# A two-layer transformer block: the feed-forward in the planner's order, weight transfers behind gate rows, the residual factor inside the residual, and adds moved between two engines

## Chip, cores and metric

The kernel runs on one core of a Trainium2 chip. The time is device microseconds from launch to end, and smaller is better. A core has TensorE (PE, the matmuls), VectorE (DVE), ScalarE (ACT), GpSimd (POOL) and SyncE (SP, whose queue issues nearly all transfers). Each works through a list of instructions of its own in order and waits for the others by semaphores.

## What is computed

A two-layer block over 512 latent tokens and 256 context tokens of width 1024, in float32. Cut to what matters here:

```
for i in range(2):
    mods = silu(c) @ w_ada[i] + b_ada[i]          # shifts, scales, gates (latent); the same for the context
    hx = x * (1 + sc1) + sh1
    ax = window_attention(hx) if i == 0 else differential_attention(hx)   # ends in a product with wo
    x  = layer_norm(alpha * x + g1 * ax, ln1_g, ln1_b)
    h  = x * (1 + sc2) + sh2
    fx = square(relu(h @ w1)) @ w2                # w1 1024x4096, w2 4096x1024
    x  = layer_norm(alpha * x + g2 * fx, ln2_g, ln2_b)
    # layer 0 does the same to the context tokens; layer 1 leaves them out
return x
```

`alpha` is 4 ** 0.25.

## The kernel before

**Tiles.** The 768 tokens are six blocks of 128 (`tb` 0 to 5; blocks 4 and 5 are context; layer 1 ends with four). Each product is made in three matmuls (lines 330, 331, 332) from a rounded half and a remainder of both operands. So each weight tile that a transfer brings as `w_raw` is cast on ACT to `w_h` and split on DVE to `w_l` (`wsplit`, lines 313 and 319), and activations likewise.

**Feed-forward.** `mlp_pipe` forms `h` for the w1 tiles 0 to 5 plainly (the function `plain`, with `relu`, its square and the split `hid`), and then the tiles q = 3 to 15 in pairs with sums of operands (`hx_sum`, `w_half`), one matmul tile fewer a pair. Products with w2 (`y_ps`) run between them; their sums are kept in `fx`. In layer 0 the tensor `acc`, which holds the LayerNorm's result, takes the residual early: `residual` (from `R0.step`) multiplies by a row of `lnrow` and adds another, and the result is spilled to memory and loaded again for the end. At the end `last_y` forms the last products. `fold` multiplies `fx` by the gate row `g` and adds it to `acc` on POOL, 24 operations; `gated_add` multiplies the last product by the gate (`g_tmp`) and adds it to `acc`. Then `stats`, `moments` (with `rstd`, a power on POOL) and `normalise` (line 540) on DVE make the LayerNorm, and `ln_job` transposes each block on PE (`xn_t`, eight transposes, line 555) and writes the next operand (`hx0m`, `hx` or `hx1m`).

**What sets the order.** A planner, `Flow`, runs through generators (jobs) while the program is built. It holds a model time `fl.T` of PE and of four more engines. A job yields a condition, and goes on when the model says that it holds; the first job that can go on is taken. PE's instructions stand exactly in the planner's order. For ACT ("A"), DVE ("D") and POOL ("G") the planner keeps a queue too, but its order binds only while `fl.pin` names the engine; otherwise the compiler's scheduler sets it. Before, "DAG" is pinned in both attentions and nothing in the feed-forwards, including the LayerNorms at their ends. `LNLAT` is what the planner adds to the end of a normalise before it lets PE transpose. An operation that carries no `ins` is planned but never pinned.

**Transfers.** All go through `dma` on SP's queue. `queue["behind"]` names an instruction behind which the following transfers must stand. Before, `plain` asks for its w1 tile (`wsplit(t["w1"][l, ft])`) at the moment of use, and the compiler places it.

**Residual rows.** The rows `g` of `lnrow` are loaded again over the gate rows (`reload`), then multiplied by alpha on DVE (`scale_inplace`, a `TENSOR_SCALAR` on 128x1024); this happens to two rows in each layer.

Of the kernel before, what the change touches and what calls it, by code (L numbers as in the profile page):

```python
# [240 lines left out]
def hybrid_block(ctx: ExitStack, tc: tile.TileContext, t: dict, out: bass.AP):  # L241
# [63 lines left out]
    def wsplit(src, n=1024, raw=None, hl=None, pool=False):  # L305
# [8 lines left out]
        a = fl.op("A", act(n), [q, hg], ins=last["cast"])  # L314
# [3 lines left out]
        else:  # L318
            last["split"] = nc.vector.tensor_tensor(**kw)  # L319
# [379 lines left out]
    def scale_inplace(ap, s):  # L699
        dv(D // 2, [], nc.vector.tensor_scalar, out=ap, in0=ap, scalar1=s, scalar2=None, op0=ALU.mult)  # L700

    def mlp_pipe(l, hx, ready, ntok, acc, get_gates, done, fx, T, R):
# [252 lines left out]
        def last_y():  # L955
            def final(half, tb, pt, p, slot):
                r = gated_add(R.pool, lambda x: sm_.give(slot, x), acc[tb], half, pt, p, gates[0 if tb < NXB else 1],
                              half == 1 if l else half == 0 or tb == ntb - 1)
# [1175 lines left out]
```

## Time and profile before

| | us |
|---|---|
| median of 3 runs (1641.33 to 1644.98) | 1643.1 |
| the profiled execution, whole | 1639.2 |
| its span in the profile | 1637.4 |
| PE busy, share of the span | 96% |
| DVE busy | 70% |
| ACT busy | 48% |
| POOL busy | 26% |
| DMA engines, mean share | 33% |

Times below count from the span's start. In the trace, attention of layer 0 goes to about 302, the second half of its out projection to 345, its feed-forward to 868 (the pairs from 445), LayerNorm and layer 1's products for attention to 915, attention to 1255, out projection and LayerNorm to 1283, and layer 1's feed-forward from 1276 to the end. A timeline row reads: start, duration, engine, source line, operation, output and inputs, shape, and in brackets the idle time of the engine before it and what ended it. A row with "x2" is two instructions together. Durations of neighbours overlap a little, so what one costs its engine is the distance between starts.

### The profile page before, as it was taken

The numbers are of one execution on the slowest core, as the hardware profiler recorded it, in microseconds if no ns is written. First come the engines' busy times: TensorE is split into PE (matmuls) and PEld (weight loads), VectorE is DVE, ScalarE is ACT, GpSimd is POOL, SyncE is SP. The second block draws the span as 40 slices with busy tenths as digits, with TensorE's granted clock in tenths as the row PEclk, the third lists the DMA queues.
The fourth block names the chain that finished last, engine by engine and source line by source line (L and its number), as shares of the span: only waits on it lengthen the run. The fifth ranks groups of instructions, "written<-read, shape, count | busy, mean of one in ns | idle before, by whom it ended". The sixth has DMA issues, their size and how long they took to land.

```text
span 1637.4 us, 25213 instructions
## 1 busy us (share of the span) xinstructions
PE 1571.6 (96%) x9465; PEld 1377.9 (84%) x9465; DVE 1142.4 (70%) x2201; ACT 791.2 (48%) x1679; POOL 433.7 (26%) x369
## 2 busy tenths in 40 slices
PE   7999999989999999999997999999999799999998
PEld 5887677779888888888986999999987788888896
DVE  4655676589686777967576677777765876566667
ACT  3465665365334334333425555556552745544450
POOL 1344453102111211121183122220100123223363
PEclk9999999999999999999998999999999899999999
DMA  9111551533344444444332222211132333333321
GB/s 372 48 53 34 181 175 44 173 118 129 102 146 163 142 132 139 158 139 148 110 133 91 81 71 71 72 49 40 39 107 100 104 116 103 103 103 103 103 68 62
DMA packets 66435, 181.18 MB, mean 111 GB/s; under 512 B 7368, under 2 KB 13320, under 8 KB 66312
## 3 DMA queue, kind: packets, MB, share of 16 engines
q1 hardware_dynamic: 66312, 179.56, 32.6%
q8 instruction: 74, 1.21, 0.3%
q14 instruction: 49, 0.40, 0.1%
HBM read 168.49 MB, written 11.04 MB: 110 GB/s over the span
## 4 chain that ended last, share of the span: by engine, by line
PE 78%; DVE 9%; ACT 5%; POOL 3%; issue 3%; DMA 2%; SPq 0%; DVEq 0%; ACTq 0%; POOLq 0%
PE y_ps L331 9%; PE y_ps L332 9%; PE y_ps L330 9%; PE h_ps L330 7%; PE h_ps L331 7%; PE h_ps L332 7%; PE qkv_ps L330 3%; PE qkv_ps L331 3%; PE qkv_ps L332 3%; PE s_ps L1785 2%; PE o_ps L1395 2%; PE pT_ps L1413 2%; PE o_ps L1823 2%; POOL acc L273 1%; PE q_ps L330 1%
## 5 line engine op out<-in xcount | busy, mean ns | idle before, releaser
L331 PE MATMUL y_ps<-w_l,hid 128*128 128x512 f32 (+1 forms) x648 | 255.0, 393 | 1.6 <-DVE w_l L319 1.6
L330 PE MATMUL y_ps<-w_h,hid 128*128 128x512 f32 (+1 forms) x648 | 255.7, 395 | 0.6 <-DVE fx L267 0.6
L332 PE MATMUL y_ps<-w_h,hid 128*128 128x512 f32 (+1 forms) x648 | 254.9, 393 | 0.0
L319 DVE TENSOR_TENSOR w_l<-w_raw,w_h 128x1024 fp32r<-128x1024 f32 (+1 forms) x133 | 160.1, 1212 | 47.9 <-ACT w_h L313 46.4
L313 ACT CAST w_h<-w_raw 128x1024 fp32r<-128x1024 f32 (+1 forms) x133 | 131.1, 1002 | 104.8 <-PE y_ps L332 76.7
L332 PEld LDWEIGHTS y_ps<-w_h,hid 128*128 128x128 f32 x648 | 122.2, 189 | 28.6
L331 PEld LDWEIGHTS y_ps<-w_l,hid 128*128 128x128 f32 x648 | 122.3, 189 | 27.5 <-DVE w_l L319 2.9
L267 DVE TENSOR_TENSOR w_half<-w_raw,w_half 128x512 fp32r<-128x512 f32 x130 | 105.8, 824 | 54.7 <-ACT w_half L270 54.3
L330 PEld LDWEIGHTS y_ps<-w_h,hid 128*128 128x128 f32 x648 | 122.4, 189 | 25.4 <-DVE fx L267 1.0
L270 ACT CAST w_half<-w_raw 128x512 fp32r<-128x512 f32 x130 | 79.2, 621 | 128.0 <-PE h_ps L332 97.8
L330 PE MATMUL qkv_ps<-w_h,hx 128*128 128x384 f32 (+1 forms) x384 | 128.6, 335 | 3.2 <-ACT w_h L313 3.2
L273 POOL TENSOR_TENSOR w_sum<-w_raw 128x512 f32<-128x512 f32 x26 | 42.7, 1643 | 328.0 <-DMA w_raw<-in_w 265.1
L331 PE MATMUL qkv_ps<-w_l,hx 128*128 128x384 f32 (+1 forms) x384 | 123.6, 322 | 2.5 <-DVE w_l L319 2.5
L273 POOL TENSOR_TENSOR e<-e,sm 128x512 f32<-128x512 f32 (+2 forms) x96 | 93.5, 990 | 112.7 <-DVE sm L267 77.8
L332 PE MATMUL qkv_ps<-w_h,hx 128*128 128x384 f32 (+1 forms) x384 | 122.9, 320 | 0.0
L267 DVE TENSOR_TENSOR fx<-y_ps,fx 128x512 f32<-128x512 f32 x110 | 75.2, 686 | 36.1 <-PE y_ps L332 35.8
L270 ACT ACTIVATE relu<-relu 128x384 f32<-128x384 f32 (+3 forms) x104 | 69.3, 671 | 61.2 <-DVE relu L267 59.9
L273 POOL TENSOR_TENSOR rope<-rope,rope 128x256 f32<-128x256 f32 (+1 forms) x40 | 35.3, 883 | 216.3 <-DVE rope L267 138.8
L273 POOL TENSOR_TENSOR w_raw<-w_raw,w_sum 128x512 f32<-128x512 f32 x26 | 39.1, 1506 | 197.3 <-DVE w_half L267 160.4
L678 DVE CUSTOM_DVE_ANT_0 w_raw<-w_raw,cB 128x512 f32<-128x512 f32 x112 | 84.0, 784 | 4.7 <-PE y_ps L332 4.1
L270 ACT ACTIVATE e<-e,nm 128x513 f32<-128x513 f32 (+2 forms) x96 | 65.9, 687 | 30.8 <-DVE nm L267 26.8
L330 PEld LDWEIGHTS qkv_ps<-w_h,hx 128*128 128x128 f32 x384 | 72.8, 189 | 5.7 <-ACT w_h L313 3.6
(268 smaller groups left out, 4315.1 us busy)
## 6 DMA issues: line engine op xcount, KB each, us to landing
w_raw<-in_w SPq DMA_DIRECT2D x128, 512.0 KB, 3.6
w_raw<-in_w_adaT SPq DMA_DIRECT2D x56, 512.0 KB, 3.8
w_raw<-in_w_ada SPq DMA_DIRECT2D x24, 512.0 KB, 4.0
w_raw<-in_b_w SPq DMA_DIRECT2D x32, 384.0 KB, 3.9
raw<-in_w_ada SPq DMA_DIRECT2D x16, 512.0 KB, 9.6
w_raw<-in_a_wq SPq DMA_DIRECT2D x8, 512.0 KB, 8.7
w_raw<-in_a_wo SPq DMA_DIRECT2D x8, 512.0 KB, 4.2
w_raw<-in_b_wo SPq DMA_DIRECT2D x8, 512.0 KB, 4.5
```

Source lines behind the costliest of these rows:

```text
L267: return fl.op("D", dve(n), deps, lat, fn(**kw))
L270: return fl.op("A", act(n), deps, lat, fn(**kw))
L273: return fl.op("G", us, deps, lat, fn(**kw))
L313: last["cast"] = nc.scalar.copy(out=h[:, :n], in_=raw[:, :n])
L319: last["split"] = nc.vector.tensor_tensor(**kw)
L330: nc.tensor.matmul(out=o, lhsT=lh, rhs=rh, start=start, stop=False, **kw)
L331: nc.tensor.matmul(out=o, lhsT=lh, rhs=rl, start=False, stop=False, **kw)
L332: last["pe"] = nc.tensor.matmul(out=o, lhsT=ll, rhs=rh, start=False, stop=stop, **kw)
L678: i = fn(**kw)
L1395: nc.tensor.matmul(out=po[odd * HD:odd * HD + HD, 0:256], lhsT=vv[:, kb, kvh], rhs=pt_[:, odd * 256:odd * 256 + 256], start=(i == 0), stop ...
L1413: nc.tensor.transpose(out=pp[:, c * P:(c + 1) * P], in_=es[j][:, i * P:(i + 1) * P], identity=ident)
L1785: nc.tensor.matmul(out=sp[:, c * 512:c * 512 + 384], lhsT=qTt[:, tt, hl, qb * P:(qb + 1) * P], rhs=kS[:, tt, c * 384:c * 384 + 384], start ...
```

## The change

- `LNLAT` falls from 6.0 to 0.2, so the planner puts a block's transposes earlier into PE's order.
- `fl.pin` is "DAG" in layer 0's feed-forward. From the end of its plain part on, `fl.loose` leaves out the weights' casts and splits and those of the halves. In layer 1's feed-forward "DAG" holds to the end of the plain part and then nothing is pinned.
- A helper `w1` asks for each w1 tile one tile ahead; the first three of layer 0 must stand on SP's queue behind the gate rows and the `acc` loads.
- `residual` applies alpha itself, in two `SCALAR_TENSOR_TENSOR`, and the four scalings of rows are left out. In layer 0 the residual gets a low priority in the plan.
- Layer 0's last adds of the second half (blocks 0 to 4) go from POOL to DVE, and the planner is told that they come after the folds.

```diff
-LNLAT = 6.0
+LNLAT = 0.2
+LOW = 100
...
-        t.eng, t.us, t.seq = eng, us, self.n
-        for d in deps:
+        t.eng, t.us, t.seq = eng, us, self.n + LOW * self.low
+        for d in flat(deps):
...
-        a = fl.op("A", act(n), [q, hg], ins=last["cast"])
+        a = fl.op("A", act(n), [q, hg], ins=None if fl.loose else last["cast"])
...
-            d = fl.op("D", dve(n), [a], ins=last["split"])
+            d = fl.op("D", dve(n), [a], ins=None if fl.loose else last["split"])
...
+        m = [m, *more]
         if last:
-            return dv(512, [m], nc.vector.tensor_tensor, out=acc[:, cs_], in0=acc[:, cs_], in1=tm, op=ALU.add)
-        return gp(pool2(512), [m], nc.gpsimd.tensor_tensor, out=acc[:, cs_], in0=acc[:, cs_], in1=tm, op=ALU.add)
+            return dv(512, m, nc.vector.tensor_tensor, out=acc[:, cs_], in0=acc[:, cs_], in1=tm, op=ALU.add)
+        return gp(pool2(512), m, nc.gpsimd.tensor_tensor, out=acc[:, cs_], in0=acc[:, cs_], in1=tm, op=ALU.add)
...
-    def residual(acc, g, b, after=None):
-        d = dv(D, [], behind(nc.vector.tensor_tensor, after), out=acc, in0=acc, in1=g, op=ALU.mult)
-        return dv(D, [d], nc.vector.tensor_tensor, out=acc, in0=acc, in1=b, op=ALU.add)
+    def residual(acc, g, b, deps, after=None):
+        d = dv(D, deps, behind(nc.vector.scalar_tensor_tensor, after), out=acc, in0=acc, scalar=ALPHA, in1=g, op0=ALU.mult,
+               op1=ALU.mult)
+        return dv(D, [d], nc.vector.scalar_tensor_tensor, out=acc, in0=b, scalar=ALPHA, in1=acc, op0=ALU.mult, op1=ALU.add)
...
+    def w1(l, ft):
+        if ft < 6 and (l, ft) not in W1:
+            kept = queue["behind"]
+            if l == 0 and ft < 3:
+                queue["behind"] = queue["w1"]
+            W1[l, ft] = wsplit(t["w1"][l, ft])
+            queue["behind"] = kept
+        return W1.get((l, ft))
...
                     if n == 0:
+                        W[ft] = w1(l, ft)
+                        w1(l, ft + 1)
...
-                        W[ft] = wsplit(t["w1"][l, ft])
...
-                              half == 1 if l else half == 0 or tb == ntb - 1)
+                              half == 1 or l == 0, more=[folds[half, tb]])
...
         if l == 0:
             y_weights(0, 1)
+        if l == 0:
+            fl.loose = True
+        else:
+            fl.pin = ""
...
-    fl.pin = ""
+    fl.pin = "DAG"
...
             dma(512, [], out=acc[tb][:, 0:512], in_=y_spill[tb])
+        queue["w1"] = queue["last"]
...
         def done1(tb, st, r):
+            if tb == NTB - 2:
+                fl.low = True
+                w1(0, 0)
+                w1(0, 1)
+                fl.low = False
             fl.add(ln_job(pool, acc[tb], tb, hx, A, B, ready, st, r, fx[tb]), 0)
...
-                d = residual(acc[tb], gx, gc, last["pe"])
+                fl.low = True
+                d = residual(acc[tb], gx, gc, rows + [fl.pe(0.0)], last["pe"])
+                fl.low = False
...
-            for b_, i in ((gx, 0), (gc, 1)):
-                reload(b_, lnrow[0, i:i + 1])
-                scale_inplace(b_, ALPHA)
+            rows[:] = [reload(b_, lnrow[0, i:i + 1]) for b_, i in ((gx, 0), (gc, 1))]
...
-                          LNLAT if tb < NTB - 1 else 2.5), 0)
+                          LNLAT), 0)
...
-    fl.pin = ""
+    fl.pin = "DAG"
...
-        scale_inplace(lb, ALPHA)
...
         def done3(tb, st, r):
+            if tb == NXB - 2:
+                w1(1, 0)
...
-            reload(gx, lnrow[1, 0:1])
-            scale_inplace(gx, ALPHA)
-            res = [lambda tb=tb: residual(acc[tb], gx, lb, last["pe"]) for tb in range(NXB)]
+            row = reload(gx, lnrow[1, 0:1])
+            res = [lambda tb=tb: residual(acc[tb], gx, lb, [row], last["pe"]) for tb in range(NXB)]
```

PE's list has as many matmuls as before. Between the transposes of blocks 4 and 5 behind layer 0's out projection stand 24 `h_ps` matmuls before and 60 now, and at the end of layer 0 block 0's transposes stand 36 `y_ps` matmuls earlier. In layer 1 the transposes come behind 78 `y_ps` matmuls of the out projection, and then 18 and 6 between blocks, where 102 stood ahead of three blocks together.

DVE's list at the last LayerNorm behind layer 0's out projection (`acc_3735` is block 5, `acc_3730` block 0, `g_3736` and `g_3738` the rows); before:

```order
L267 SCALAR_TENSOR_TENSOR acc_3735<-acc_3735,g_tmp 128x512
L678 TENSOR_TENSOR acc_3730<-acc_3730,g_3736 128x1024
L267 BN_STATS bn<-acc_3735 128x6
L267 TENSOR_TENSOR hx0m<-fx,hx0m 128x2x128
L267 TENSOR_SCALAR g_3738<-g_3738 128x1024
L267 BN_AGGR mv<-bn 128x2
L267 TENSOR_TENSOR hx0m<-fx,hx0m 128x2x128
L267 TENSOR_SCALAR rstd<-mv 128x1
L267 TENSOR_TENSOR hx0m<-fx,hx0m 128x2x128
L540 TENSOR_SCALAR acc_3735<-acc_3735,mv,rstd 128x1024
```

and now:

```order
L272 BN_STATS bn<-acc_3735 128x6
L272 TENSOR_TENSOR hx0m<-fx,hx0m 128x2x128
L272 BN_AGGR mv<-bn 128x2
L272 TENSOR_SCALAR rstd<-mv 128x1
L272 TENSOR_TENSOR hx0m<-fx,hx0m 128x2x128 x2
L684 SCALAR_TENSOR_TENSOR acc_3730<-acc_3730,g_3736 128x1024
L545 TENSOR_SCALAR acc_3735<-acc_3735,mv,rstd 128x1024
L272 SCALAR_TENSOR_TENSOR acc_3730<-g_3738,acc_3730 128x1024
```

The scaling of the row (`TENSOR_SCALAR g_3738`) is gone, and the only residual operation left ahead of block 5's normalise is a product between it and its `rstd` step. The w_l splits of w1 tiles, three of which stood together ahead of block 4's normalise, are now spread.

DVE's list where the plain part ends (`w_l` from here on are w2 tiles; `hx0m` with 4x128 are sums that write over part of the operand of the plain part); before:

```order
L267 TENSOR_TENSOR hid<-relu,hid 128x768
L267 TENSOR_TENSOR hx_sum<-fx,hx_sum 128x4x128 x2
L319 TENSOR_TENSOR w_l<-w_raw,w_h 128x1024 x2
L267 TENSOR_TENSOR w_half<-w_raw,w_half 128x512
L319 TENSOR_TENSOR w_l<-w_raw,w_h 128x1024
L267 TENSOR_TENSOR relu<-relu 128x768
L267 TENSOR_TENSOR hid<-relu,hid 128x768
L267 TENSOR_TENSOR hx0m<-fx,hx0m 128x4x128 x3
L319 TENSOR_TENSOR w_l<-w_raw,w_h 128x1024
```

and now:

```order
L272 TENSOR_TENSOR hx_sum<-fx,hx_sum 128x4x128
L272 TENSOR_TENSOR hid<-relu,hid 128x768
L272 TENSOR_TENSOR hx_sum<-fx,hx_sum 128x4x128
L272 TENSOR_TENSOR hx0m<-fx,hx0m 128x4x128 x3
L324 TENSOR_TENSOR w_l<-w_raw,w_h 128x1024 x3
L272 TENSOR_TENSOR relu<-relu 128x768
L272 TENSOR_TENSOR hid<-relu,hid 128x768
L324 TENSOR_TENSOR w_l<-w_raw,w_h 128x1024
```

The three `hx0m` sums moved ahead of the first three w2 splits.

POOL's list at the end of layer 0 (`fx` with a gate row `g`, then `acc` with `fx`, are the folds); before:

```order
L273 TENSOR_TENSOR acc_7899<-acc_7899,fx 128x512
L273 TENSOR_TENSOR acc_7900<-acc_7900,fx 128x512
L273 TENSOR_TENSOR fx<-fx,g_7997 128x512 x2
L273 TENSOR_TENSOR acc_7901<-acc_7901,fx 128x512
L273 TENSOR_TENSOR acc_7902<-acc_7902,fx 128x512
L273 TENSOR_TENSOR acc_7897<-acc_7897,g_tmp 128x512
L273 TENSOR_TENSOR rstd<-rstd,mhalf 128x1
L273 TENSOR_TENSOR acc_7898<-acc_7898,g_tmp 128x512
L273 TENSOR_TENSOR rstd<-rstd,mhalf 128x1
```

and now:

```order
L278 TENSOR_TENSOR fx<-fx,g_7993 128x512 x2
L278 TENSOR_TENSOR acc_7897<-acc_7897,fx 128x512
L278 TENSOR_TENSOR acc_7898<-acc_7898,fx 128x512
L278 TENSOR_TENSOR fx<-fx,g_7995 128x512 x2
L278 TENSOR_TENSOR acc_7899<-acc_7899,fx 128x512
L278 TENSOR_TENSOR acc_7900<-acc_7900,fx 128x512
L278 TENSOR_TENSOR rstd<-rstd,mhalf 128x1 x6
```

The adds of `g_tmp` are gone from POOL, and the six `rstd` follow the last fold directly.

More of the change, by code (lines that the diff above doesn't have):

```diff
@@ L60, in __init__, with flat @@
         self.done, self.ins = None, None
+def flat(x):
+    return [z for y in x for z in flat(y)] if isinstance(x, (list, tuple)) else [x]
 class Flow:
@@ L74, in __init__ @@
         self.events = []
-        self.prev, self.order, self.pin = {}, None, ""
+        self.prev, self.order, self.pin, self.loose, self.low = {}, None, "", False, False
     def pe(self, us):
@@ L521, in reload @@
     def reload(b, src, c0=0):
-        dma(D - c0, [], out=b[:, c0:], in_=src[:, c0:].broadcast_to([P, D - c0]))
+        return dma(D - c0, [fl.pe(0.0)], out=b[:, c0:], in_=src[:, c0:].broadcast_to([P, D - c0]))
     def stats(a, half, dep, st=None):
@@ L583, in hxs, with gated_add @@
         return hx[k // 2][:, k % 2, hl, sl]
-    def gated_add(pool, give, acc, half, pt, p, gate, last, scale=1.0):
+    def gated_add(pool, give, acc, half, pt, p, gate, last, scale=1.0, more=()):
         cs_ = slice(half * 512, (half + 1) * 512)
@@ L752, in half @@
                 w = R.half_tile(nhalf[0] - 1)
-                a = ac(512, [dep, R.rhalf.get()], nc.scalar.copy, out=w[:, 0:512], in_=src)
-                d = dv(512, [a], nc.vector.tensor_tensor, out=w[:, 512:1024], in0=src, in1=f(w)[:, 0:512],
-                       op=ALU.subtract)
+                a = nc.scalar.copy(out=w[:, 0:512], in_=src)
+                a = fl.op("A", act(512), [dep, R.rhalf.get()], ins=None if fl.loose else a)
+                d = nc.vector.tensor_tensor(out=w[:, 512:1024], in0=src, in1=f(w)[:, 0:512], op=ALU.subtract)
+                d = fl.op("D", dve(512), [a], ins=None if fl.loose else d)
                 rel = Task()
@@ L895, in pair @@
             yield from mix(3)
-        gates, st, Wy, fresh = [], {}, {}, set()
+        gates, st, Wy, fresh, folds = [], {}, {}, set(), {}
         def y_weights(c, half, n=2):
@@ L920, in fold @@
             d = gp(pool2(512), [d], nc.gpsimd.tensor_tensor, out=x, in0=x, in1=g[:, cs_], op=ALU.mult)
-            gp(pool2(512), [d], nc.gpsimd.tensor_tensor, out=acc[tb][:, cs_], in0=acc[tb][:, cs_], in1=x, op=ALU.add)
+            folds[half, tb] = gp(pool2(512), [d], nc.gpsimd.tensor_tensor, out=acc[tb][:, cs_], in0=acc[tb][:, cs_], in1=x,
+                                 op=ALU.add)
         def sink(c, half, tb, pt, p, slot):
@@ L957, in final @@
                 r = gated_add(R.pool, lambda x: sm_.give(slot, x), acc[tb], half, pt, p, gates[0 if tb < NXB else 1],
-                              half == 1 if l else half == 0 or tb == ntb - 1)
+                              half == 1 or l == 0, more=[folds[half, tb]])
                 st[tb], r = stats(acc[tb], half, r, st.get(tb))
-                r_half[tb] = r
+                first_half, r_half[tb] = r_half.get(tb), r
                 if half:
-                    done(tb, st[tb], r)
+                    done(tb, st[tb], [first_half, r])
             early, r_half = [], {}
@@ L1029, in last_y @@
                     sm_.give(slot, m)
-                    r = dv(256, [m], nc.vector.tensor_tensor, out=acc[tb][:, cs_], in0=acc[tb][:, cs_], in1=tm, op=ALU.add)
+                    r = dv(256, [m, folds[1, tb]], nc.vector.tensor_tensor, out=acc[tb][:, cs_], in0=acc[tb][:, cs_], in1=tm,
+                           op=ALU.add)
                     r = dv(256, [r], nc.vector.bn_stats, out=parts[:, n + 1], in_=acc[tb][:, cs_])
@@ L1500, in hybrid_block @@
         acc = [apool_top.tile([P, D], F32, name="acc0", tag="acc", bufs=NTB) for _ in range(NTB)]
+        rows = []
         gx, gc = [bcast_load(pool, gate_d[(0, 2)][s:s + 1], f"g1{s}", 512, 2) for s in range(2)]
@@ L1630, in hybrid_block @@
         EB1, XB1, SB = 5, 3, 1
-        fl.prev, fl.pin = {}, "DAG"
+        fl.loose = False
+        fl.pin = "DAG"
         rsk, rsq = Ring(fl, SB), Ring(fl, SB)
@@ L1971, in hybrid_block @@
         fl.run()
-    fl.pin = ""
+    fl.pin = "DAG"
     with tc.tile_pool(name="mlp1", bufs=1, reuse_waits="tile") as pool:
```

1 line of the change is left out of this document (added).

## The prediction

> **What bounds the kernel now.** I read the page first, then the windows by stage, then the waits and the timelines of TensorE (PE) and VectorE (DVE) in the stages where PE is not full.
>
> ```profile
> span 1637.4 us, 25213 instructions
> PE 1571.6 (96%) x9465; PEld 1377.9 (84%) x9465; DVE 1142.4 (70%) x2201; ACT 791.2 (48%) x1679; POOL 433.7 (26%) x369
> 302.50:360.00 57.50, 51.97 (x263) 43.60 (x262) 41.17 (x76) 31.24 (x77) 4.20 (x6) 0.95 0.54 188
> 339.20:399.90 60.70, 55.17 (x351) 53.37 (x350) 57.29 (x79) 34.78 (x70) 10.42 (x5) 0.94 0.34 123
> 445.00:826.00 381.00, 373.75 (x1852) 333.58 (x1851) 283.89 (x538) 148.16 (x237) 69.98 (x47) 1.00 0.44 145
> 826.00:915.00 89.00, 78.41 (x364) 65.91 (x363) 55.58 (x95) 33.27 (x87) 47.37 (x37) 0.94 0.26 89
> 1255.00:1325.00 70.00, 61.05 (x352) 53.35 (x352) 59.65 (x95) 40.16 (x83) 8.39 (x8) 0.93 0.24 78
> 1325.00:1637.40 312.40, 304.54 (x1868) 271.62 (x1867) 204.63 (x275) 143.11 (x253) 114.77 (x72) 1.00 0.29 96
> ```
>
> In a window's row stand its length, the busy time of PE, weight loads, DVE, ScalarE (ACT) and GpSimd (POOL), and the granted clock. PE is busy 1571.6 of 1637.4 us, so all its idle time is 65.8 us. The change adds no matmul and takes none away, so it can only gain idle time and slow clock. Both lie in the three stages round a LayerNorm that feeds PE: out projection into feed-forward of layer 0 (57.50 − 51.97 = 5.53 us idle, clock 0.95), the end of layer 0 (89.00 − 78.41 = 10.59, clock 0.94) and layer 1's LayerNorm before its feed-forward (70.00 − 61.05 = 8.95, clock 0.93). The middle of layer 0's feed-forward (381.00 − 373.75 = 7.25 in 381 us) and layer 1's (7.86 in 312) are nearly full.
>
> **Stage 1: out projection, LayerNorm, first feed-forward tiles (302 to 406).**
>
> ```profile
> 343.19 1.03 PE L555 MATMUL xn_t<-identr,acc 128*128 128x128 f32 x8
> 356.46 1.94 PE L555 MATMUL xn_t<-identr,acc 128*128 128x128 f32 x8 [5.17 <-issue]
> 405.79 0.39 PE L330 MATMUL y_ps<-w_h,hid 128*128 128x512 f32 x1
> 349.80 0.68 DVE L267 SCALAR_TENSOR_TENSOR acc<-acc,g_tmp 128x512 f32<-128x512 f32 x1
> 350.40 1.22 DVE L678 TENSOR_TENSOR acc<-acc,g 128x1024 f32<-128x1024 f32 x1
> 351.54 0.68 DVE L267 BATCH_NORM_STATS2 bn<-acc 128x6 f32<-128x512 f32 x1
> 352.14 0.41 DVE L267 TENSOR_TENSOR hx0m<-fx,hx0m 128x256 fp32r<-128x256 f32 x1
> 353.61 0.69 DVE L267 TENSOR_SCALAR g<-g 128x1024 f32<-128x1024 f32 x1 [1.06 <-DMA g<-in_lnrow]
> 355.55 0.81 DVE L540 TENSOR_SCALAR acc<-acc,mv,rstd 128x1024 f32<-128x1024 f32 x1 [0.44 <-POOL rstd L273]
> 371.43 0.95 DVE L267 TENSOR_TENSOR relu<-relu 128x768 f32<-128x768 f32 x1
> 372.30 1.22 DVE L267 TENSOR_TENSOR acc<-acc,g 128x1024 f32<-128x1024 f32 x1
> 381.57 1.75 DVE L267 TENSOR_TENSOR relu<-relu 128x768 f32<-128x768 f32 x1 [0.23 <-ACT relu L270]
> 383.24 3.49 DVE L267 TENSOR_TENSOR fx<-fx 128x512 f32<-128x512 f32 x2
> 397.55 2.34 DVE L319 TENSOR_TENSOR w_l<-w_raw,w_h 128x1024 fp32r<-128x1024 f32 x2
> ```
>
> The 5.17 us of PE are the last block's LayerNorm: a residual product (350.40), a 1.06 us DMA wait and a scaling (353.61) stand in DVE's queue ahead of its normalise (355.55). After the idle time eight transposes take 1.94 us instead of 1.03. In the changed order the scaling vanishes, the wait for the second row comes behind that normalise, the residual product stands between block 5's rstd step and its normalise, where DVE waits for POOL anyway (0.44), and 60 h matmuls instead of 24 stand between the transposes of blocks 4 and 5. The normalise then starts near 355.55 − 1.06 − 0.6 − 0.44 = 353.4 and ends near 354.2. PE is through with the out projection at 345.4 (343.19, 0.8 of transposes, six matmuls), and block 4's transposes (0.9) and 60 h matmuls of 256 columns at 0.117 (half of a 512's 0.233, below) bring it to 353.3. So of 5.17 some 0.9 stays. PE's own gain by the first y matmul is then the idle 5.53 − 0.9 plus slow clock, 0.05 × 57.5 = 2.9, and a little behind 360: **8 us at most**.
>
> What is late next is DVE. It is busy 57.29 of 60.70 us from 339.20 to 399.90, and the residuals are still to be done before the first w2 splits (397.55, two of them). Counted from the changed order, between the first residual and those splits stand 12 residual operations and 4 w_l splits of 1024 columns, 10 of 768, 25 of 512, 4 of 256 and a normalise (by their rows 0.41 and 0.81 at most, 2.5 together). By start-to-start spacing a 1024 costs 1.14 (350.40 to 351.54), a 768 0.87 (371.43 to 372.30), a 512 0.60 (351.54 to 352.14): 16 × 1.14 + 10 × 0.87 + 25 × 0.60 + 2.5 = 44.4, and 1.14 for the first w2 split, 45.5. From a first residual at about 350.0 (today's is at 350.40, and one split less now stands ahead of it) DVE is through at 395.5. Beside POOL such operations are slower: 383.24 took 3.49 for two (1.2 alone) and 381.57 took 1.75 (0.95), together 3.1. That gives 398.6 for the split and the first y matmul, instead of 405.79: **gain 7.2**. Without contention PE's 8 bounds it; with today's 3.41 us of DVE idle kept as well (60.70 − 57.29) it is 4.0. I take 7.2, since those POOL operations stay. The two scalings that go (0.69 each) are inside this count. The trace has no `scalar_tensor_tensor` of 1024 columns; the 512 one at 349.80 gives way after 0.60, as other 512s do, so twelve of 1024 cost between 1.14 and 1.20 each, 0.7 in all, within these ends. The third DVE piece shown with the change costs PE at least 1.7 us, already covered by the 398.6: the hx0m sums now stand ahead of the w2 splits and need PE's last tile partly read.
>
> The w1 transfers now go behind gate rows and acc loads, so the gate row no longer waits behind three 512 KB transfers. That lets block 0's chain begin earlier. I value it at nothing of its own, since PE does not wait for it in 302 to 345; if a w1 tile came late instead, DVE would have it within the bounds above.
>
> **The middle (406 to 826).**
>
> ```profile
> PE h_ps L330 <- ACT relu L270: 3.1, 2, 1.6
> 462.87 0.44 PE L330 MATMUL h_ps<-hx_sum,w_half 128*128 128x384 f32 x1 [1.48 <-ACT relu L270]
> 656.83 0.44 PE L330 MATMUL h_ps<-hx_sum,w_half 128*128 128x384 f32 x1 [1.61 <-ACT relu L270]
> ```
>
> Pinning DVE, ACT and POOL to the plan moves their rows here by seven places at most, and PE's order is the same. The waits for relu (3.1 in all, two times) can vanish, gain 3, or come in two or three more of the 13 pairs, loss 4.  Value **0**, from −4 to +3.
>
> **Stage 2: end of layer 0 (826 to 915).**
>
> ```profile
> 813.16 0.33 SPq L279 DMA_DIRECT2D w_raw<-in_w  x1
> 826.10 3.27 POOL L273 TENSOR_TENSOR fx<-fx,g 128x512 f32<-128x512 f32 x2 [28.36 <-DMA g<-gate_d]
> 862.23 1.29 POOL L273 TENSOR_TENSOR acc<-acc,g_tmp 128x512 f32<-128x512 f32 x1
> 864.76 0.55 POOL L273 TENSOR_TENSOR rstd<-rstd,mhalf 128x1 f32<-128x1 f32 x1 [1.24 <-DVE rstd L267]
> 868.56 0.60 PE L555 MATMUL xn_t<-identr,acc 128*128 128x128 f32 x4
> 880.23 2.17 PE L555 MATMUL xn_t<-identr,acc 128*128 128x128 f32 x8 [2.76 <-DVE g_tmp L589]
> 892.58 0.45 PE L330 MATMUL qkv_ps<-w_h,hx 128*128 128x384 f32 x1 [2.93 <-ACT w_h L313]
> 894.45 0.69 PE L331 MATMUL qkv_ps<-w_l,hx 128*128 128x384 f32 x1 [1.42 <-DVE w_l L319]
> 869.96 1.84 DVE L540 TENSOR_SCALAR acc<-acc,mv,rstd 128x1024 f32<-128x1024 f32 x1
> 859.67 0.40 PE L331 MATMUL y_ps<-w_l,hid 128*128 128x512 f32 x1
> 859.90 0.39 PE L332 MATMUL y_ps<-w_h,hid 128*128 128x512 f32 x1
> ```
>
> A 512-wide matmul starts every 0.233 us (859.67 to 859.90). Block 0's transposes move 36 matmuls forward, 8.4 us: from 868.56 to 860.2. But POOL does 24 fold operations from 826.10 to 862.23 (1.5 us each), and in the changed order all six rstd stand behind them. So block 0 gets its rstd at 862.23 + 0.55 and its normalise (0.81) ends near 863.9: a **new wait of 3.8**. From there the five removed POOL adds (1.29 each; on DVE about 0.7, and no hand-over) shorten each block's chain. I count the later blocks just in time, the last at about 894, and the two qkv waits (2.93, 1.42) gone, because the weights' cast and split no longer queue behind late blocks. Idle is then 3.8 plus some 0.5, instead of 10.59: gain 6.3. The clock lost 0.06 × 89 = 5.3 us before; after a 3.8 us wait I expect two thirds of it again, gain 1.7. **Gain 8.0**. If the qkv waits stay it is 3.7; if the folds run at the 1.3 us of the add at 862.23, they end at 857 and the new wait is gone: 11.8. I take 8.0, since today's folds run at 1.5.
>
> The clock shows in the transposes: 2.17 us for eight behind a 2.76 us wait. [...]
>
> The adds moved to DVE can meet a fold: at 869.96 a normalise beside a POOL add took 1.84 instead of 0.81. [...]
>
> **Stage 3: layer 1's LayerNorm (1255 to 1325).**
>
> ```profile
> 1276.21 0.58 PE L330 MATMUL h_ps<-hx1m,w_h 128*128 128x256 f32 x1 [1.64 <-ACT hx1m L270]
> 1278.73 0.58 PE L331 MATMUL h_ps<-hx1m,w_h 128*128 128x256 f32 x1 [1.94 <-DVE hx1m L267]
> 1297.51 0.39 PE L330 MATMUL h_ps<-hx1m,w_h 128*128 128x256 f32 x1 [1.52 <-ACT relu L270]
> 1305.42 0.39 PE L330 MATMUL h_ps<-hx1m,w_h 128*128 128x256 f32 x1 [2.03 <-ACT relu L270]
> ```
>
> The transposes of blocks 0 and 1 now stand 24 and 6 y matmuls earlier, so the first h matmuls find their operand nearly ready: of 1.64 + 1.94 I take 2.5 as gone. The relu waits (1.52, 2.03) stay; their order does not change. With 1 us of clock the **gain is 3.5**: 0 if the same chain is merely waited for sooner, 6 if all hx1m waits and half the clock loss of 0.07 × 70 go. Two scalings of 0.69 leave DVE here, inside this value. The rest of layer 1 keeps its order: 0.
>
> **Sum.** 7.2 + 0 + 8.0 + 3.5 = 18.7. The profiled execution took 1639.2 us, so 1620.5; the median of the runs is 1643.1, 3.9 above it, so **1624**.
>
> **Rivals.**
> - A, DVE eats stage 1 (chance 0.12). DVE is at 94% from 339 to 400, and pinned to an order it cannot slip w2 splits ahead; a late second row (it landed at 353.6) would now hold up all behind it. If the first y matmul stays at 405.79, 11.5 remains: 1632. Against it: two scalings are gone, and the row is wanted no sooner than today.
> - B, the fold chain sets stage 2 (0.10). The gate row stands on the SP queue behind a weight transfer (813.16) that waits for a DVE split to free its buffer. If that moves forward less than PE, the new wait grows by up to the 7.2 of stage 1, and 18.7 − 7.2 = 11.5 remains: 1632. For it: POOL's 28 us idle ends with that DMA. Against: the split it hangs on moves with PE.
> - C, slower (0.10). The pins hold ACT's relu behind another operation in each pair of the middle, as at 462.87. There are 13 pairs and two have the wait today. Eleven more of 1.55 and about 1 us of slow clock each make 28; less 18.7, about 9 slower: 1652. It decides from 1.7 us (18.7/11) a pair, clock included. For it: the pins hold in the whole feed-forward except for weights. Against: ACT is busy 148 of 381 us there, and the rows hardly move.
> - D, no change (0.07). The planner's 6.0 us for a LayerNorm was right, and earlier transposes only wait sooner: some 1.5 us at each of the twelve in layer 0 gives back 18 and leaves 1642. Against: by the rows above a product and an add (0.60 each), statistics (0.68), rstd (0.55) and normalise (0.81) make 3.2, near 4 with the small steps, under the 5.6 us of 24 matmuls.
>
> **How the numbers follow.** The forecast has 0.61, with its own range from the bounds: 4.0 − 4 + 3.7 + 0 = 3.7 to 8 + 3 + 11.8 + 6 = 28.8, that is 1614 to 1639. With A and B inside, 1612 to 1640 should hold the time 8 times in 10; most of C and D lies above. About 0.2% (3.3 us) is what a measurement can tell from no change. Faster: forecast, A, B, 0.83; same: D, 0.07; slower: C, 0.10.
>
> **What would show it.** Right: no 5 us wait ahead of block 5's transposes; a first y matmul 6 to 8 us earlier, with DVE full before it; one wait of 3 to 5 us at the first transposes of layer 0's end, behind POOL; no qkv wait for a weight. Wrong: waits for relu in many pairs, a span from first y to first fold that grows, or folds that begin later against PE.

## The result, and the profile after

The changed kernel takes **1628.0 us** (median of 4 runs, 1625.8 to 1628.5) against 1642.4 for the one before in the same comparison: a ratio of 0.9907, 95% interval 0.9890 to 0.9925. That is 14.4 us faster, where 18.7 was worked out; the time lies in the range, 4 us above the number given. The sum came out, but several of its reasons did not, as the experiments show. One of the four executions of pins_off below took 2175.9 us at a granted clock of 0.656, so its median is that of the other three.

The windows of the changed kernel, with the bounds of those shown of before (its line numbers are 5 higher for the same helper lines):

```profile
span 1626.7 us, 25214 instructions
PE 1570.4 (97%) x9465; PEld 1376.0 (85%) x9465; DVE 1144.1 (70%) x2202; ACT 790.2 (49%) x1679; POOL 443.5 (27%) x364
302.50:360.00 57.50, 56.63 (x302) 47.01 (x303) 40.72 (x72) 30.31 (x76) 3.44 (x6) 0.97 0.52 180
339.20:399.90 60.70, 60.70 (x394) 58.82 (x393) 58.01 (x80) 34.01 (x70) 14.09 (x6) 1.00 0.35 126
445.00:826.00 381.00, 372.64 (x1839) 332.49 (x1838) 282.25 (x537) 145.66 (x234) 66.36 (x46) 1.00 0.44 144
826.00:915.00 89.00, 83.61 (x431) 71.76 (x430) 63.85 (x117) 41.46 (x107) 43.17 (x34) 0.96 0.27 89
1255.00:1325.00 70.00, 62.91 (x395) 56.10 (x394) 55.89 (x88) 44.07 (x92) 22.14 (x7) 0.97 0.27 84
```

PE's idle time falls from 5.53 to 0.87 us in the first window, from 10.59 to 5.39 in the one at layer 0's end, and from 8.95 to 7.09 in layer 1's; the clock rises by 0.02 to 0.04 in each. From 339 to 400 us PE now has no idle time at all. DVE is a little fuller than before, 58.01 of 60.70 against 57.29.

PE's timeline shows the main waits that are left (at transposes, at the first w2 product, and the longest of layer 1):

```profile
323.15 1.06 PE L560 MATMUL xn_t<-identr,acc 128*128 128x128 f32 x8 [0.86 <-PE y_ps L337]
357.03 1.04 PE L560 MATMUL xn_t<-identr,acc 128*128 128x128 f32 x8
401.78 0.50 PE L335 MATMUL y_ps<-w_h,hid 128*128 128x512 f32 x1 [0.62 <-ACT w_h L318]
403.04 0.50 PE L336 MATMUL y_ps<-w_l,hid 128*128 128x512 f32 x1 [0.76 <-DVE w_l L324]
864.36 1.97 PE L560 MATMUL xn_t<-identr,acc 128*128 128x128 f32 x8 [4.23 <-DVE acc L545]
1324.46 0.58 PE L335 MATMUL h_ps<-hx_sum,w_half 128*128 128x256 f32 x1 [3.04 <-ACT relu L275]
```

The 5.17 us ahead of block 5's transposes (357.03) are gone. The new wait at block 0's transposes at the end of layer 0 is 4.23 us (3.8 was worked out), and eight transposes behind it take 1.97. POOL's rows say why:

```profile
860.03 2.92 POOL L278 TENSOR_TENSOR acc<-acc,fx 128x512 f32<-128x512 f32 x2
862.91 0.54 POOL L278 TENSOR_TENSOR rstd<-rstd,mhalf 128x1 f32<-128x1 f32 x1
```

The first rstd follows the last fold, and block 0's normalise (DVE `acc`, L545) needs that rstd, as the prediction said.

### The profile page after: what moved, and what is told of

Same layout as the page of the kernel before. It is cut to its first block, busy times and chain, and to the rows that moved or that the text cites. A ratio compares the mean times of both kernels' runs of the same rounds, so it can differ in the third digit from the quotient of the medians.

```text
span 1626.7 us, 25214 instructions
## 1 busy us (share of the span) xinstructions
PE 1570.4 (97%) x9465; PEld 1376.0 (85%) x9465; DVE 1144.1 (70%) x2202; ACT 790.2 (49%) x1679; POOL 443.5 (27%) x364
## 4 chain that ended last, share of the span: by engine, by line
PE 48%; DVE 6%; POOL 4%; ACT 2%; issue 2%; DMA 1%; SPq 0%; DVEq 0%; POOLq 0%; ACTq 0%
PE y_ps L335 6%; PE y_ps L336 6%; PE y_ps L337 6%; PE h_ps L335 5%; PE h_ps L336 5%; PE h_ps L337 5%; PE qkv_ps L335 3%; PE qkv_ps L336 3%; PE qkv_ps L337 3%; PE s_ps L1819 2%; PE o_ps L1857 2%; POOL acc L278 1%; PE pT_ps L1885 1%; POOL w_raw L278 1%; DVE acc L272 1%
## 5 line engine op out<-in xcount | busy, mean ns | idle before, releaser
L278 POOL TENSOR_TENSOR w_raw<-w_raw,w_sum 128x512 f32<-128x512 f32 x26 | 52.4, 2016 | 187.2 <-DVE w_half L773 169.6
L684 DVE CUSTOM_DVE_ANT_0 w_raw<-w_raw,cB 128x512 f32<-128x512 f32 x112 | 90.0, 831 | 15.6 <-PE y_ps L337 13.9
L275 ACT ACTIVATE relu<-relu 128x768 f32<-128x768 f32 (+3 forms) x104 | 69.6, 671 | 49.8 <-DVE relu L272 48.9
```

The lines of the kernel that those rows point to most:

```text
L275: return fl.op("A", act(n), deps, lat, fn(**kw))
L278: return fl.op("G", us, deps, lat, fn(**kw))
L684: i = fn(**kw)
```

## The experiments

Two theories stood at the start. The first: the gain lies in PE's order at the LayerNorms (LNLAT) and the shorter adds. The rival: the pins carry it. To compare stages I use start times of PE's rows in the profiles. **S1** runs from the first matmul of the out projection's second half in layer 0 to the first `y_ps` of its feed-forward; **middle** from there to the gate's transposes (`gate_t`, near 707); **S2** from those to the first `qT_ps` of layer 1's attention; **L1** from layer 1's first out projection matmul to PE's last row. Between S2 and L1 stand 289.7 to 290.6 us in every profile. "Start" is the time at which S1 begins. Times are medians in us; the ratio is to the kernel before, run beside it. Each stage time is from a single profiled execution.

| kernel | time | ratio, 95% interval | start | S1 | middle | S2 | L1 |
|---|---|---|---|---|---|---|---|
| before | 1642.4 | | 302.5 | 103.3 | 301.0 | 208.0 | 424.6 |
| before_again | 1644.7 (one) | | 303.8 | 103.8 | 303.4 | 209.5 | 424.4 |
| changed | 1628.0 | 0.9907 (0.9890 to 0.9925) | 304.1 | 97.7 | 303.1 | 201.1 | 422.9 |
| after_again | 1627.0 | 0.9899 (0.9886 to 0.9913) | 304.7 | 97.1 | 304.2 | 199.4 | 421.7 |
| pins_off | 1626.0 | 0.9896 (0.9881 to 0.9912) | 303.5 | 100.9 | 301.7 | 200.2 | 419.7 |
| pool_adds | 1629.9 | 0.9920 (0.9906 to 0.9935) | 303.3 | 97.0 | 304.8 | 199.8 | 424.0 |
| lnlat_alone | 1647.5 | 1.0022 (1.0012 to 1.0033) | 304.0 | 114.4 | 303.3 | 203.3 | 423.2 |
| w1_back | 1653.1 | 1.0062 (1.0049 to 1.0074) | 302.5 | 119.1 | 303.1 | 199.4 | 430.3 |
| w1_nohold | 1630.5 | 0.9928 (0.9913 to 0.9942) | 303.4 | 101.8 | 304.1 | 200.8 | 421.7 |
| scale_back | 1636.1 | 0.9958 (0.9943 to 0.9973) | 303.4 | 101.4 | 304.5 | 199.1 | 428.1 |
| lnlat_pins_back | 1630.3 | 0.9927 (0.9913 to 0.9940) | 303.7 | 102.3 | 301.3 | 198.1 | 425.6 |
| lnlat_pins_adds_back | 1640.6 | 0.9984 (0.9971 to 0.9997) | 303.5 | 101.3 | 305.8 | 206.6 | 424.2 |
| pin_plain0 | 1623.4 | 0.9879 (0.9866 to 0.9893) | 303.1 | 95.7 | 304.5 | 200.3 | 419.7 |
| plain0_ln2 | 1620.9 | 0.9865 (0.9848 to 0.9881) | 302.1 | 95.7 | 304.0 | 198.2 | 421.2 |

**The two kernels once more (after_again, before_again), no edit.**

> The changed kernel once more, for a second profile. Theory 1 (the gain lies at the LayerNorm stages): median 1626 to 1630, again about 14 us under the kernel before; the first y matmul of layer 0 starts 97 to 98 us after the out projection's second half starts (97.7 in the first profile of the changed kernel, 103.2 in the one of before), and block 0's transposes at the end of layer 0 wait about 4 us. Rival (the first profile was a chance one: its out projection began 1.6 us later than before's and with slow matmuls): that offset differs by more than 1 us here, and the stage times differ by more than 1 us too.

> The kernel before once more, for a second profile, to tell a stage's change from chance. If the 1.6 us by which the changed kernel's out projection of layer 0 starts later is chance, it starts here at 302 to 305 us; if it belongs to the change, at 302.5 again. Stage times: first y matmul 103 us after that start, 301 us more to the gate's transposes at 707, 208 from there to the first transposes of layer 1's queries, within 1 us each.

The time was again under before, by 16 us (14 in the first comparison), and block 0's transposes at the end of layer 0 waited 5.08 us, where about 4 was expected. The start of S1 scatters from 302.1 to 304.7 over all the profiles, before_again's 303.8 among them, so nothing shows that the late start in the first profile of the changed kernel belongs to the change. The middle scatters too, from 301.0 to 305.8, pinned or not. The expectation that each stage repeats within 1 us missed for the middle (2.4) and for S2 (1.5 in the kernel before, 1.7 in the changed one). S1 and S2 repeat within 1 to 2 us, so only differences above that are read below.

**The pins (pins_off).** PE's and POOL's lists stay the same. (`fl.prev` holds the last instruction of each pinned engine; it is emptied where the pins begin again.)

```diff
-    fl.pin = "DAG"
+    fl.pin = ""
     def need(*lms):
...
-        fl.pin = "DAG"
+        fl.prev, fl.pin = {}, "DAG"
...
-    fl.pin = "DAG"
+    fl.pin = ""
     with tc.tile_pool(name="mlp1", bufs=1, reuse_waits="tile") as pool:
```

> The changed kernel with nothing pinned in the feed-forwards, as before; PE's and POOL's lists stay the same, only DVE, ACT and 27 transfers move. Theory 1 (the gain comes from PE's order and the shorter adds, the pins are worth nothing or cost the 1.4 us of waits for w_h and w_l at the first y matmul): 1624 to 1630. Rival 2 (the pins carry the gain, because without them DVE puts residuals and splits ahead of the LayerNorm chains, as before at 350 us): 1633 to 1641, and waits of several us at the transposes of blocks 3 to 5.

1626.0: the pins as a whole are worth nothing in this set, so the rival falls. But two stages move against each other. S1 is 3 to 4 us longer without them, and block 5's transposes wait again, as the row shows. L1 is 2 to 3 us shorter.

```profile
358.06 1.94 PE L560 MATMUL xn_t<-identr,acc 128*128 128x128 f32 x8 [2.54 <-issue]
```

**LNLAT alone (lnlat_alone), made from the kernel before.**

```diff
-LNLAT = 6.0
+LNLAT = 0.2
...
-                          LNLAT if tb < NTB - 1 else 2.5), 0)
+                          LNLAT), 0)
```

> The kernel before with LNLAT 0.2 only: transposes earlier in PE's list, nothing pinned, w1 transfers, scalings and POOL adds as before. Theory 1: the wait of 5.2 us ahead of block 5's transposes shrinks and the stages at the LayerNorms gain part, 1632 to 1639. Rival 2 (without the pins earlier transposes only wait sooner): 1640 to 1648. Rival 3 (LNLAT alone carries all): 1626 to 1631.

1647.5, at the far end of rival 2's range: earlier transposes alone make the kernel slower. S1 is 114.4 instead of 103.5. PE's timeline there:

```profile
327.08 1.94 PE L555 MATMUL xn_t<-identr,acc 128*128 128x128 f32 x8 [5.56 <-DMA acc<-y_spill]
365.37 1.94 PE L555 MATMUL xn_t<-identr,acc 128*128 128x128 f32 x8 [8.91 <-ACT w_h L313]
```

Block 0 waits 5.56 and block 5 waits 8.91. The brackets name a load and ACT's `w_h`, but the transposes need the block's normalised `acc`, and both times they begin within 0.1 us of the end of DVE's normalise (326.97 and 365.27); that `w_h` ended at 364.37. DVE's rows:

```profile
321.37 0.69 DVE L589 TENSOR_TENSOR g_tmp<-y_ps,g 128x512 f32<-128x512 f32 x1 [6.96 <-DMA g<-gate_d]
326.16 0.81 DVE L540 TENSOR_SCALAR acc<-acc,mv,rstd 128x1024 f32<-128x1024 f32 x1
360.43 1.18 DVE L319 TENSOR_TENSOR w_l<-w_raw,w_h 128x1024 fp32r<-128x1024 f32 x1
361.99 0.69 DVE L267 TENSOR_SCALAR g<-g 128x1024 f32<-128x1024 f32 x1 [0.39 <-DMA g<-in_lnrow]
364.46 0.81 DVE L540 TENSOR_SCALAR acc<-acc,mv,rstd 128x1024 f32<-128x1024 f32 x1 [0.44 <-POOL rstd L273]
```

Block 0's chain waits 6.96 us for the gate row, and with DVE unpinned a weight split and the scaling of a row still stand ahead of block 5's normalise. S2 is 203.3 instead of 208.8, so at the end of layer 0 the same edit does win some 5 us.

**The w1 transfers (w1_back, w1_nohold).** First, w1 is asked for at use again; then only the hold behind the gate rows is taken out.

```diff
-                        W[ft] = w1(l, ft)
-                        w1(l, ft + 1)
+                        W[ft] = wsplit(t["w1"][l, ft])
...
-                w1(0, 0)
-                w1(0, 1)
+                pass
...
-                w1(1, 0)
+                pass
```

> The changed kernel with the w1 transfers placed as before, three of them ahead of the gate rows on SP's queue. Theory 1 (revised: earlier transposes are worth nothing in stage 1 unless the gate row and the acc loads come first; in the kernel with LNLAT alone block 0's transposes waited 5.6 us for an acc load): block 0's transposes wait 4 to 6 us here too, 1630 to 1634. Rival (the order of the w1 transfers is worth nothing, the pins hold the rest): 1626 to 1629.

```diff
-            if l == 0 and ft < 3:
-                queue["behind"] = queue["w1"]
```

> The changed kernel with w1 tiles asked for one tile ahead, but without the hold behind the gate rows: only SP's list moves, three 512 KB transfers stand ahead of the gate rows again. Theory 1 (the place on SP's queue matters only for block 0: in the kernel with w1 as before its gate row ended a 6.8 us wait of DVE at 319 and its transposes waited 4.5 us; the other 20 us there came from splits pinned late): out projection to first y matmul 101 to 103 us instead of 97 to 98, 1630 to 1633. Rival (the hold carries the 26 us): 1645 to 1653. Rival (it is worth nothing): 1626 to 1628.

w1_back takes 1653.1, slower than the kernel before, and far outside both expectations. w1_nohold takes 1630.5 with an S1 of 101.8, as expected of the place on SP's queue alone. So the hold is worth some 3 us (1630.5 against 1628.0 and 1627.0) and asking early, with the pins, some 22 (1653.1 against 1630.5). In w1_back the plan puts a tile's cast and split at the moment of use, and the pins hold ACT and DVE to that. PE's rows there, and the window's row:

```profile
378.74 0.45 PE L335 MATMUL h_ps<-hx0m,w_h 128*128 128x384 f32 x1 [1.90 <-ACT w_h L318]
381.37 0.44 PE L337 MATMUL h_ps<-hx0m,w_l 128*128 128x384 f32 x1 [2.02 <-DVE w_l L324]
393.20 0.44 PE L335 MATMUL h_ps<-hx0m,w_h 128*128 128x384 f32 x1 [2.02 <-ACT w_h L318]
394.46 0.44 PE L337 MATMUL h_ps<-hx0m,w_l 128*128 128x384 f32 x1 [0.65 <-DVE w_l L324]
380.00:400.00 20.00, 15.96 (x71) 15.33 (x72) 18.06 (x21) 4.77 (x7) 6.14 (x3) 0.83 0.23 80
```

Two tiles show it here, each with a wait for `w_h` and another for `w_l`, and the clock falls to 0.83 (third number from the end in the window's row, 1.00 in the changed kernel from 339 to 400). Layer 1, where `w1` is edited too, loses 8 us (L1 430.3 against 422.9 and 421.7) with waits for `w_h` and `w_l` as well. Whether it would cost as much without the pins was not run. In w1_nohold the gate row lands late (DVE waits 6.55 for it, 2.61 in the changed kernel), and block 0's transposes wait 4.17:

```profile
320.35 0.69 DVE L594 TENSOR_TENSOR g_tmp<-y_ps,g 128x512 f32<-128x512 f32 x1 [6.55 <-DMA g<-gate_d]
325.09 1.94 PE L560 MATMUL xn_t<-identr,acc 128*128 128x128 f32 x8 [4.17 <-DVE acc L545]
```

**The factor in the residual (scale_back).**

```diff
-    d = dv(D, deps, behind(nc.vector.scalar_tensor_tensor, after), out=acc, in0=acc, scalar=ALPHA, in1=g, op0=ALU.mult,
-           op1=ALU.mult)
-    return dv(D, [d], nc.vector.scalar_tensor_tensor, out=acc, in0=b, scalar=ALPHA, in1=acc, op0=ALU.mult, op1=ALU.add)
+    d = dv(D, deps, behind(nc.vector.tensor_tensor, after), out=acc, in0=acc, in1=g, op=ALU.mult)
+    return dv(D, [d], nc.vector.tensor_tensor, out=acc, in0=acc, in1=b, op=ALU.add)
...
+            for b_, r_ in zip((gx, gc), list(rows)):
+                rows.append(dv(D // 2, [r_], nc.vector.tensor_scalar, out=b_, in0=b_, scalar1=ALPHA, scalar2=None,
+                               op0=ALU.mult))
...
+        scale_inplace(lb, ALPHA)
...
+            row = dv(D // 2, [row], nc.vector.tensor_scalar, out=gx, in0=gx, scalar1=ALPHA, scalar2=None, op0=ALU.mult)
```

> The changed kernel with the residual as two tensor_tensor operations and the four scalings of rows back on DVE. Theory 1 (four times 0.69 us of DVE, two of them in the full stage ahead of the first y matmul, where PE and not DVE ended last by 0.6 us): 0 to 1.5 us, 1626 to 1629. Rival (DVE is the bound there, and pinned scalings wait for the row's transfer with all behind them): 1630 to 1634.

1636.1: 8 to 9 us slower, even more than the rival said. Four scalings are 2.8 us of DVE; the rest is mostly waiting. The plan moves PE's order a little too: 72 `h_ps` matmuls instead of 60 stand ahead of block 5's transposes, which wait 2.85 all the same. DVE's rows of that kernel, one in each layer, and PE's row behind the second:

```profile
355.64 0.69 DVE L272 TENSOR_SCALAR g<-g 128x1024 f32<-128x1024 f32 x1 [2.44 <-DMA g<-in_lnrow]
1273.40 0.69 DVE L272 TENSOR_SCALAR g1x<-g1x 128x1024 f32<-128x1024 f32 x1 [3.78 <-DMA g1x<-in_lnrow]
1274.01 0.69 DVE L272 TENSOR_TENSOR acc<-acc,g_tmp 128x512 f32<-128x512 f32 x1
1274.61 1.22 DVE L324 TENSOR_TENSOR w_l<-w_raw,w_h 128x1024 fp32r<-128x1024 f32 x1
1275.88 0.58 PE L337 MATMUL h_ps<-hx1m,w_l 128*128 128x256 f32 x1 [4.63 <-DVE w_l L324]
```

A scaling waits for its row's transfer, and the add, the statistics and the weight's split that stand behind it on DVE wait too. PE then waits 4.63 us for that split.

**The adds (pool_adds, lnlat_pins_back, lnlat_pins_adds_back).** pool_adds takes the changed kernel and puts the adds back:

```diff
-                              half == 1 or l == 0, more=[folds[half, tb]])
+                              half == 1 if l else half == 0 or tb == ntb - 1, more=[folds[half, tb]])
```

> The changed kernel with layer 0's last five adds on POOL again, behind the folds. Theory 1 (the adds on DVE shorten each block's chain by POOL's hand-over, and are most of stage 2's gain): stage 2 loses 4 to 8 us, 1632 to 1636, with waits for xn_t in several blocks. Rival (the folds' end sets stage 2 whichever engine adds): 1627 to 1630.

1629.9, inside the rival's range, with S2 unchanged (199.8); the interval overlaps the changed kernel's. Theory 1 missed: there the adds on DVE do not win stage 2. lnlat_pins_back takes LNLAT and the pins back at once (LNLAT 6.0 with the pins kept was not run):

```diff
-LNLAT = 0.2
+LNLAT = 6.0
...
-                          LNLAT), 0)
+                          LNLAT if tb < NTB - 1 else 2.5), 0)
```

and the three edits of pins_off.

> The changed kernel with LNLAT 6.0 (2.5 for the last block) and no pins in the feed-forwards: left of the change are the w1 order, the residual and the adds on DVE. Theory 1 (LNLAT is needed for all three stages): 1637 to 1643, with PE waits at the transposes of blocks 5 and of layer 0's end much as before. Rival (the w1 order, the residual and the adds carry the gain without LNLAT): 1626 to 1632.

1630.3, so theory 1 falls as far as it says that LNLAT is needed everywhere. S2 is 198.1, no longer than in the changed kernel, with no long wait at a transpose; S1 is 102.3, only about 1 us better than before. Against pins_off, which differs from it by LNLAT alone, it is 4 us slower (1630.3 and 1626.0): LNLAT wins 1.4 in S1 and 5.9 in L1 there, and loses 2.1 in S2. Then the adds go back as well (the edit of pool_adds on top):

> The kernel with LNLAT and pins as before, and now the last five adds on POOL too: left of the change are the w1 order and the residual. Theory 1 (the adds on DVE are what won stage 2 there, 198 us from the gate's transposes to layer 1's first query transposes instead of 208 to 210; earlier transposes win the same time in another way): this stretch is back at 205 to 210, and the time at 1637 to 1642. Rival (stage 2 was won by the order of transfers and residuals): 198 to 200, 1629 to 1632.

1640.6, S2 206.6, and before's waits return:

```profile
873.70 0.75 PE L560 MATMUL xn_t<-identr,acc 128*128 128x128 f32 x4 [2.00 <-POOL rstd L278]
883.88 0.76 PE L560 MATMUL xn_t<-identr,acc 128*128 128x128 f32 x4 [2.77 <-DVE g_tmp L594]
```

So in S2 either edit wins what there is to win: the adds on DVE (8.5 us, 206.6 to 198.1), or, with the adds on POOL, the earlier transposes together with the rest (199.8). Both together win no more.

**A better version (pin_plain0, plain0_ln2).** The pins win in S1 and lose in L1, so pin_plain0 ends them where layer 0's plain part ends:

```diff
-        if l == 0:
-            fl.loose = True
-        else:
-            fl.pin = ""
+        fl.pin = ""
...
-    fl.pin = "DAG"
+    fl.pin = ""
     with tc.tile_pool(name="mlp1", bufs=1, reuse_waits="tile") as pool:
```

> The changed kernel pinned only from the out projection to the end of layer 0's plain part, and nowhere in the feed-forwards behind it. Theory 1 (the pins win about 2.5 us ahead of the first y matmul, where block 5's transposes waited 2.5 us without them, and lose 2 us in the middle and some in layer 1 by waits for relu and w_h): 1622 to 1625. Rival (the pins make no difference anywhere, and the differences between single profiles are chance): 1626 to 1628.

1623.4, as expected: S1 95.7, L1 419.7. Each of its four runs (up to 1624.5) is faster than each of the changed kernel's (from 1625.4), though the intervals still touch. The middle is no shorter (304.5), so what was said of it there is not borne out. plain0_ln2 has the long latency again, at the end of layer 0 alone:

```diff
-                          LNLAT), 0)
+                          6.0 if tb < NTB - 1 else 2.5), 0)
```

> The kernel pinned only to the end of layer 0's plain part, with the LayerNorm latency 6.0 (2.5 for the last block) at the end of layer 0 alone. Theory 1 (there the transposes come too early, 3.8 us ahead of the folds' end, while with the long latency that stretch was 1 to 2 us shorter): 1620 to 1623, no wait over 1 us at block 0's transposes. Rival (the wait hides work that is late in any case): 1623 to 1626.

1620.9, ratio 0.9865 (0.9848 to 0.9881): the wait of 3.8 us at block 0's transposes is gone and S2 is 2 us shorter. A wait of 2.3 us at a y matmul came instead. The interval overlaps that of pin_plain0, so the last 2.5 us rest on one stage of one profile and the medians, and are not shown. This is 1.35% under the kernel before and faster than the changed one.

## Why the prediction was right, and where it was not

The total is in part luck: the 7.2 of stage 1 was DVE's count, where PE's own bound of 8 lies close by; stage 3's 2.2 is a larger gain of the transposes less a loss by the pins; and the w1 transfers, put at nothing, are what the rest needs. The means of two profiles each give the sum: S1 −6.1 (103.5 to 97.4), middle +1.4, S2 −8.6 (208.8 to 200.2), L1 −2.2 (424.5 to 422.3), start +1.2, together −14.3, as in the medians.

- **Stage 1, 7.2 forecast, 6.1 measured.** The size was right, the reason only in part. "What is late next is DVE" failed as the bound: PE is busy 60.70 of 60.70 us from 339 to 400, and only then waits 0.62 for `w_h` and 0.76 for `w_l`. So PE's own bound, "8 us at most", decided, with the weights' casts and splits 1.4 us behind it. Those waits come from the `hx0m` sums ahead of the w2 weights, which the prediction saw in the lists and put at 1.7 us or more. ACT casts the sums when PE is done with their operand, and the weights' casts follow:

```profile
399.11 1.66 ACT L275 CAST hx0m<-fx 128x512 fp32r<-128x512 f32 x3 [2.01 <-PE h_ps L337]
400.68 2.94 ACT L318 CAST w_h<-w_raw 128x1024 fp32r<-128x1024 f32 x3
```

In pin_plain0, whose pins end there, a `w_l` split stands at 394.60, ahead of these sums, the waits are gone, and S1 is 95.7, that is 7.8 us under before. The lower end of the term has a slip: 398.6 with 3.41 us of idle time added leaves a gain of 3.8, not 4.0.

- **The w1 transfers, valued at nothing of their own**, were mis-sized most: "PE does not wait for it in 302 to 345" is true of before, where block 0's transposes stood 24 matmuls later. With earlier transposes the hold is worth some 3 us, and with the pins asking early is worth some 22. Without both, the rest of the change is slower than the kernel before (1653.1 against 1642.6).
- **The residual's factor, "inside this count" with 0.69 us each**, is worth 8 to 9 us with DVE pinned; unpinned it was not run. Its price was not the operation but its place: it is the first to wait for a row's transfer. For the wait that goes from 353.61 the prediction had this; for layer 1 it had only the 0.69.
- **The middle, 0**: the profiles scatter by 4.8 us there, and pinned and unpinned ones lie on both sides. The two relu waits, 3.1 us before, became three of 1.49, 0.63 and 0.43, and no gain. Rival C (a relu wait in every pair) did not come; its 1 us of slow clock a pair was the author's estimate, and in the kernel before the granted clock is 1.00 in the 3 us behind each of the two relu waits (from 462.87 and from 656.83).
- **Stage 2, 8.0 forecast, 8.6 measured**, with the new wait of 4.23 for 3.8, and the qkv waits nearly gone (0.31 and 0.55 left). The clock's loss came near the two thirds that were the author's estimate (0.04 × 89 = 3.6 us, of 5.3 before). The fold chain did set block 0. That the adds on DVE shorten the chain was right without LNLAT (8.5 us) and idle with it.
- **Stage 3, 3.5 forecast, 2.2 measured**: the earlier transposes win more (5.9 between lnlat_pins_back and pins_off; 4.8 against before, 424.5 to 419.7), and the pins give 2.6 of it back (422.3 against 419.7), the 3.04 us wait for relu at 1324 among it. pins_off and pin_plain0 do not have that wait. Of the two relu waits that were to stay (1.52, 2.03), 1.52 and 0.69 are left; this new one was not foreseen. It begins on POOL, as the last section shows.
- **Rivals A, B and D** did not come. D's mechanism, transposes that only wait sooner, did come in stage 1 of lnlat_alone, at blocks 0 and 5.

## What to carry to other kernels

In a pinned order an operation that waits for a transfer makes all behind it wait (in scale_back a scaling waited 3.78 us for its row, and PE 4.63 us for a split behind it). So what precedes it (transfers asked for early, rows that need no extra pass) was worth far more here than its busy time: 8 to 9 us for four operations of 0.69, and some 22 for weights asked for one tile ahead. Price an edit that belongs to a set in the presence of the others: LNLAT alone was 4 us slower than before and 4 us faster in the presence of the other edits without pins; the adds were worth 8.5 us of S2 without LNLAT and the pins, and nothing with them. Pin where the planned order wins and let go where it doesn't; that alone gave some 4 us more here.

## What was not expected of the hardware

A short POOL operation was held up for long beside a DVE that was never idle. One add of 128x512 on POOL took 14.94 us in the changed kernel and 1.63 in pins_off:

```profile
1307.54 14.94 POOL L278 TENSOR_TENSOR w_raw<-w_raw,w_sum 128x512 f32<-128x512 f32 x1 [6.79 <-ACT hx1m L275]
1307.50:1321.30 13.80, 13.80 (x84) 11.98 (x82) 13.80 (x18) 4.22 (x8) 13.76 (x1) 1.00 0.22 76
1322.51 0.62 ACT L771 CAST w_half<-w_raw 128x512 fp32r<-128x512 f32 x1 [8.93 <-POOL w_raw L278]
1299.98 1.63 POOL L278 TENSOR_TENSOR w_raw<-w_raw,w_sum 128x512 f32<-128x512 f32 x1 [0.69 <-POOL w_raw L278]
```

The first three rows are of the changed kernel, the last is of pins_off. DVE is busy 13.80 of 13.80 us in that stretch, and the add ends (1322.48) in DVE's next pause (1321.35 to 1323.16). ACT's cast waits 8.93 us for it, the copy of relu stands behind that cast, and PE waits the 3.04 us at 1324. The same add took 14.94 us in after_again, pool_adds, w1_nohold and scale_back as well, each time with a wait of 3.0 to 3.1 on PE. That the unbroken run on DVE is the cause fits these rows; no run changed it by itself.

Executions of one program scatter by stage: the middle of layer 0 took from 301.0 to 305.8 us in 14 profiles in which PE's order there hardly differs. The kernel before, run twice, differs by 2.4 us with the same number of matmuls:

```profile
405.80:706.80 301.00, 294.18 (x1437) 259.76 (x1437) 227.73 (x458) 112.43 (x181) 55.24 (x37) 1.00 0.43 139
407.60:711.00 303.40, 295.70 (x1437) 261.28 (x1436) 226.96 (x458) 112.48 (x181) 55.05 (x37) 0.99 0.42 137
```

PE is idle 0.9 us longer in the second and busy 1.5 us longer, at a granted clock of 0.99 instead of 1.00. Over the 14 profiles the idle time there goes from 6.8 to 8.6 us and the clock from 1.00 to 0.99. Why the clock falls there in one execution and not in another stays open.

In these profiles the length of one wait alone does not decide whether the clock falls. Eight transposes took 1.94 us behind a wait of 2.54 (pins_off, above), but not behind one of 2.85 in scale_back. The windows' rows give the granted clock behind each, 0.50 in pins_off and 1.00 in scale_back:

```profile
358.10:359.90 1.80, 1.80 (x9) 1.80 (x10) 1.80 (x2) 0.71 (x3) 0.00 (x0) 0.50 0.69 280
360.38 1.09 PE L560 MATMUL xn_t<-identr,acc 128*128 128x128 f32 x8 [2.85 <-DVE acc L545]
360.40:361.40 1.00, 1.00 (x9) 1.00 (x10) 1.00 (x2) 0.32 (x1) 0.00 (x0) 1.00 0.02 8
```

What does decide it, these runs do not show.
